# Hyena transforms by the time index modulo 4, with half the products, the lo parts of five weight streams by accumulating DMAs, and new DMA figures in the planner

## The chip, the cores and the metric

The kernel runs on one core of one Trainium2 chip. The metric is the device time of one execution in microseconds (us), the median over several runs. A core has TensorE (PE, with its weight loads shown as PEld), VectorE (DVE), ScalarE (ACT), GpSimd (POOL), SyncE (SP), whose queue issues the transfers, and 16 DMA engines.

## The reference, cut to what matters

Two transformer blocks run one after the other on 512 tokens of width 1024. The first block has neighbourhood attention, a Hyena mixer, a gated merge and a SwiGLU; the second has latent attention, a state-space branch, cross attention, a gated merge and a convolved SwiGLU. The change touches the Hyena mixer. Its long convolution is a product in the frequency domain, twice in a row (orders 0 and 1), over 512 tokens and 512 channels:

```python
def long_conv_bidir(u, h_fwd, h_bwd, bias):
    B, L, C = u.shape
    k2 = jnp.concatenate([h_fwd, jnp.zeros((1, C), jnp.float32), h_bwd[:0:-1]], axis=0)
    U = jnp.fft.rfft(u.astype(jnp.float32), n=2 * L, axis=1)
    K = jnp.fft.rfft(k2, n=2 * L, axis=0)
    y = jnp.fft.irfft(U * K[None], n=2 * L, axis=1)[:, :L]
    return (y + u.astype(jnp.float32) * bias.astype(jnp.float32)).astype(u.dtype)
...
    for n in range(HY_ORDER):
        z = gates[n] * long_conv_bidir(z, filt[:, 0, n], filt[:, 1, n], bias[n])
```

The projections around it are `h @ w_in` (its columns for the Hyena inputs are `w_hy` in the kernel, those of the two gates `w_gna` and `w_ghy`, those of the context's keys `w_kvc`) and `y_hy @ w_hy_o` (`w_hyo`).

## The kernel before, in words

**Numbers in two parts.** Every weight and activation is held as a hi part, rounded to fp32r by a copy on ACT, and a lo part, the original minus hi, made by a subtraction on DVE (`split` L783, `lo` L778). A product is three matmuls: hi by hi, hi by lo, lo by hi (`mm` L788). Weights come through `stream` (L797): one 512 KB load brings a group of 8 blocks of 128x128, which is then split into two tiles of 128x1024; `proj` takes 8 blocks (24 matmuls) for one output tile of 128x512 when the input has 1024 rows.

**The planner.** The code does not issue instructions as it goes. `Trace.add` records every call with its operands, a duration (`Trace.time` L479) and what it depends on. `Trace.plan` (L691) runs a list scheduler (`schedule` L542) over the five queues, forward and backward by turns, with the figures of `LAG` (L246: how long after one engine's end another can start), `RELEASE` and the DMA rate at L495, and with 48 page pairs of 128x512 floats (`PAGES` L32) as a limited resource. The order of the best pass is what `emit` (L707) writes out. So the figures set the order in every queue of the whole program, and no instruction waits for a planned time: it waits for semaphores alone.

```python
LAG = (
...
    (1500.0, 2000.0, 1000.0, 1300.0, 2250.0),
)
...
        return max(450.0, out.size() * 4 / 360.0)
```

The last row of `LAG` is a DMA before PE, DVE, ACT, POOL and another DMA, in ns; 360 is GB/s. All transfers go out from SP's queue.

**Hyena** (`hyena` L1195). 12 tiles of 128 channels are projected with `w_hy` and run through a short convolution (`short_conv`, whose tile has two edge columns set to zero by memsets on POOL). `to_time` (L1206) turns four of them with PE into time on the partitions. Times are split by parity: p is the time modulo 2, hh the half. For each order and each half of the channels, `order` (L1237) computes, for both halves kt of the 256 odd frequencies, cosine (j=0) and sine (j=1) sums of the even and the odd times: 2 p x 2 j x 2 hh x 3 = 24 matmuls of 256 columns per kt. A sum and a difference of the two banks give frequencies k and 511-k; they are multiplied with the filters' spectrum, which `filters` (L1107) has stored in DRAM, added and subtracted once more and split. The inverse takes 48 matmuls per half. In order 0 time lies on the partitions of the result; in order 1 the operands are exchanged, so that channels do, and the gate is multiplied in two strided pieces per tile.

**What stands around it.** `hyena` is mixed with the rest of the filters, the context's keys and values (`context` L1323) and the first gate (`gate_na` L1513); after it `neighbourhood` (L1433) is mixed with `branch_hy` (L1524), which takes `w_ghy` and `w_hyo`. In the profile every instruction has line L714, the one in `emit` that issues it, so rows are told apart by engine, form and time. By the times of their loads, the filters lie in 0 to 75 us, Hyena in 75 to 220, the neighbourhood attention in 220 to 430, the merge in 430 to 560, the first feed-forward in 560 to 900, the second block's branches and merge in 900 to 1320, its feed-forward in 1320 to the end.

Of the kernel before, what the change touches and what calls it, by code (L numbers as in the profile page):

```python
# [15 lines left out]
F32 = mybir.dt.float32  # L16
# [8 lines left out]
P = 128  # L25
# [99 lines left out]
def _constants():  # L125
    c = {}
    perm = _token_perm()
    inv = (np.float32(10000.0) ** (-np.arange(16, dtype=np.float32) / np.float32(16))).astype(np.float32)
    rc, rs = np.zeros((P, T), np.float32), np.zeros((P, T), np.float32)
    for p in range(P):  # L130
        d = p % 64
        pos = (perm // 64 if d < 32 else perm % 64).astype(np.float32)
        ang = (pos * inv[d % 16]).astype(np.float64)
        rc[p] = np.cos(ang)
        rs[p] = np.sin(ang) * (-1.0 if d % 32 < 16 else 1.0)
    c["rope1"] = np.concatenate([rc, rs], 1)

    i, k = np.arange(256)[:, None], np.arange(256)[None]
    w = np.pi * (2 * k + 1) / 1024.0
    ce, co, se, so = np.cos(w * 2 * i), np.cos(w * (2 * i + 1)), np.sin(w * 2 * i), np.sin(w * (2 * i + 1))  # L140
    c["dft"] = np.concatenate(
        [m.astype(np.float32).reshape(2, P, 256).transpose(1, 0, 2).reshape(P, 512) for m in (ce, se, co, so, ce.T, se.T)], 1)
# [7 lines left out]
    c["zfeat"] = np.ascontiguousarray(z.T)  # L150
# [3 lines left out]
    tt = np.array([[2 * (hh * P + np.arange(P)) + p for hh in range(2)] for p in range(2)]).reshape(4, P)  # L154
    c["inv2"] = np.tile((f(10000.0) ** (-np.arange(0, 32, 2, dtype=f) / f(32))).astype(f)[None], (P, 1))
    c["cmask"] = np.where(np.arange(P)[None] <= np.arange(P)[:, None], 0.0, NEG).astype(f)
    c["eye16"] = np.tile(np.eye(16, dtype=f), (2, 1))
    c["decay"] = np.ascontiguousarray(decay[tt].transpose(1, 0, 2)).reshape(P, 4 * T)
    return c


def layout(inp):
# [88 lines left out]
    (1500.0, 2000.0, 1000.0, 1300.0, 2250.0),  # L251
# [4 lines left out]
RELEASE = 200.0, 150.0, 150.0, 100.0, 1200.0  # L256
TABLES = {AF.Silu: (0,), AF.Sin: (1, 0), AF.Exp: (2,), AF.Gelu_apprx_tanh: (3,)}
# [75 lines left out]
class Call:  # L333
    __slots__ = ("engines", "engine", "name", "args", "kw", "time", "rank", "deps", "then", "waits", "pieces", "begun", "urgent", "start", "number", "tables", "columns", "ports")
# [128 lines left out]
class Trace:  # L463
# [41 lines left out]
    def add(self, engines, name, args, kw):  # L505
# [25 lines left out]
        c.tables = TABLES.get(args[2]) if name == "activation" else None  # L531
        deps.discard(c.number)
# [9 lines left out]
    def schedule(self, order, back=False):  # L542
# [36 lines left out]
        while left or events:  # L579
# [78 lines left out]
            while events and events[0][0] <= now:  # L658
# [13 lines left out]
                if kind == 0:  # L672
                    idle[c.engine] = True
                    for j in c.deps if back else c.then:
                        d = calls[j]
                        gap = LAG[d.engine][c.engine] if back else LAG[c.engine][d.engines[0]]
                        n += 1
                        push(events, (now + gap, n, 2, j))
                    if not back and c.pieces:
                        n += 1  # L680
                        push(events, (now + RELEASE[c.engine], n, 1, i))
                    if not back:
                        continue
# [23 lines left out]
    def emit(self):  # L707
        at = lambda x: x.placed() if isinstance(x, View) else x
        for c in sorted(self.calls, key=lambda c: (c.start, c.number)):
# [3 lines left out]
            f = getattr(getattr(self.nc, ENGINES[c.engine]), c.name)  # L713
# [4 lines left out]
class Program:  # L718
# [78 lines left out]
    def stream(self, ap):  # L797

        for gi in range(ap.shape[0]):
# [3 lines left out]
            self.split((wh, wl), raw)  # L803
# [303 lines left out]
    def filters(self):  # L1107
# [8 lines left out]

        self.dft = lambda j, i, c0, n: tuple(w[:, i * 256 + c0 : i * 256 + c0 + n] for w in dft[j])
# [33 lines left out]
        for o in range(2):  # L1151
            for j in (1, 0):
# [17 lines left out]
                for kt in range(2):  # L1170
# [6 lines left out]
                    for r, op in enumerate((ALU.add, ALU.subtract)):  # L1177
                        K = self.u2()
                        V.tensor_tensor(out=K, in0=e, in1=O, op=op)
# [15 lines left out]
    def hyena(self):  # L1195
        nc, a = self.nc, self.a
        V = nc.vector
        blocks = self.stream(a["w_hy"])
# [38 lines left out]
        def order(o):  # L1237
            for half in range(2):
                zt = zT[half]
                PQ = []  # L1240
                for kt in range(2):
# [3 lines left out]
                    banks = []  # L1245
                    for p in range(2):
                        ps = self.psum("s")
                        for j in range(2):
                            for hh in range(2):
                                q = p * 2 + hh  # L1250
                                self.mm(ps[:, j * 256 : j * 256 + 256], self.dft(2 * p + j, hh, kt * P, P), tuple(z[:, q * 256 : q * 256 + 256] for z in zt), hh == 0, hh == 1)
                        banks.append(ps)
                    e = self.u2()
                    nc.scalar.copy(e, banks[0])
# [11 lines left out]
                    V.tensor_tensor(out=S[:, 1], in0=Yv[:, :, 0], in1=Yv[:, :, 1], op=ALU.subtract)  # L1266
                    d = (self.u4(dt=F32R), self.u4(dt=F32R))
                    self.split(d, T1)
                    PQ.append(d)
                    yield  # L1270
                pq = lambda p, j, kt, c0, n: tuple(t[:, p * 512 + j * 256 + c0 : p * 512 + j * 256 + c0 + n] for t in PQ[kt])
                inv = lambda p, j, kt, c0, n: self.dft(2 + j if p else 4 + j, kt, c0, n)
                if o == 0:
                    zn = (self.u4(dt=F32R), self.u4(dt=F32R))
                    zT[half] = zn
                    for p in range(2):
                        ps = self.psum("mm")
                        for hh in range(2):
                            n = 0
                            for j in range(2):  # L1280
                                for kt in range(2):
                                    self.mm(ps[:, hh * 256 : hh * 256 + 256], inv(p, j, kt, hh * P, P), pq(p, j, kt, 0, 256), n == 0, n == 3)
                                    n += 1
# [5 lines left out]
                else:  # L1289
                    for c in range(2):  # L1290
                        ct = half * 2 + c
                        ps = self.psum("mm")
                        for p in range(2):
                            n = 0
                            for j in range(2):
                                for kt in range(2):
                                    self.mm(ps[:, p * 256 : p * 256 + 256], pq(p, j, kt, c * P, P), inv(p, j, kt, 0, 256), n == 0, n == 3)
                                    n += 1
                        y = self.u2()
                        yv = y.rearrange("p (cb r c) -> p r cb c", cb=8, r=8)  # L1300
                        for p in range(2):
                            V.tensor_tensor(
                                out=yv[:, :, :, p : 8 : 2],
                                in0=ps[:, p * 256 : p * 256 + 256].rearrange("p (r cb c) -> p r cb c", r=8, cb=8),
                                in1=g2[ct][:, p : 512 : 2].rearrange("p (r cb c) -> p r cb c", r=8, cb=8),
# [17 lines left out]
    def context(self):  # L1323
# [4 lines left out]
        blocks = self.stream(self.a["w_kvc"])  # L1328
# [184 lines left out]
    def gate_na(self):  # L1513

        blocks = self.stream(self.a["w_gna"])
# [8 lines left out]
    def branch_hy(self):  # L1524

        nc = self.nc
        gb, ob = self.stream(self.a["w_ghy"]), self.stream(self.a["w_hyo"])
# [784 lines left out]
```

## Time and profile before

| what | us |
|---|---|
| median of 3 runs | 1740.57 (1739.26 to 1743.97) |
| the profiled execution's own time | 1740.42 |
| its span, first to last instruction | 1738.6 |
| PE busy | 1713.5 |
| DVE busy | 1176.4 |
| ACT busy | 714.2 |

The profile is of one execution. Busy times are unions of instructions on an engine; a matmul's end is modelled, so matmuls overlap in it and the pace is read from their starts.

### The profile page before, as it was taken

To read this page: it belongs to the slowest core of one execution; us is meant where nothing else is said; L and a number is where in the kernel's file an instruction comes from. 1 tells how busy PE (TensorE), PEld (TensorE's weight loads), DVE (VectorE), ACT (ScalarE), POOL (GpSimd) and SP (SyncE) were. 2 spreads that over 40 slices of the span, in tenths; PEclk is the share of its full clock that TensorE was granted. 3 is DMA by queue.
4 is the path that set the end of the run, shared out by engine and by line. 5 is a ranking of instruction groups with operands and counts; after the bars stand their busy time and mean duration, and the time that the engine had idled before them with its cause. 6 is when DMAs were issued, how large, how long until landed. Compare 5 with 4: busy or idle time off the path is not lost.

```text
span 1738.6 us, 22865 instructions
## 1 busy us (share of the span) xinstructions
PE 1713.5 (99%) x8494; PEld 1411.7 (81%) x8494; DVE 1176.4 (68%) x2452; ACT 714.2 (41%) x1185; POOL 29.0 (2%) x69
## 2 busy tenths in 40 slices
PE   7999999999999999999999999999999999999999
PEld 3589988888888888888888887888887888888887
DVE  6898976679997275453277947569987526896420
ACT  4544354566454122233162612556554313554310
POOL 0000000000000000000000000010100000000000
PEclk9999999999999999999999999999999999999999
DMA  9535323437963235323255355402356321222420
GB/s 343 171 124 170 108 88 99 144 117 256 353 231 115 80 106 173 110 73 121 73 187 179 131 171 148 132 35 93 113 191 230 110 85 61 85 73 85 144 93 19
DMA packets 93661, 235.41 MB, mean 135 GB/s; under 512 B 18316, under 2 KB 26252, under 8 KB 93550
## 3 DMA queue, kind: packets, MB, share of 16 engines
q1 hardware_dynamic: 93550, 233.95, 40.3%
q8 instruction: 67, 1.10, 0.3%
q14 instruction: 44, 0.36, 0.1%
HBM read 206.91 MB, written 27.00 MB: 135 GB/s over the span
## 4 chain that ended last, share of the span: by engine, by line
PE 89%; DVE 6%; DMA 2%; ACT 2%; issue 1%; SPq 0%; ACTq 0%; DVEq 0%
PE banks L714 89%; DVE pages L714 4%; ACT pages L714 2%; DVE small L714 1%; SPq L714 0%; DMA pages<-in_w_ada_dram 0%; DMA pages<-in_w_hyo_dram 0%; DMA pages<-in_w_out_dram 0%; DMA br<-pages 0%; DVE banks L714 0%; DMA pages<-s5w 0%; DMA ud<-pages 0%; DVE R L714 0%; ACTq L714 0%; DVEq L714 0%
## 5 line engine op out<-in xcount | busy, mean ns | idle before, releaser
L714 PE MATMUL banks<-pages,pages 128*128 128x512 f32 (+5 forms) x7769 | 1639.3, 370 | 9.2 <-DVE pages L714 7.8
L714 PEld LDWEIGHTS banks<-pages,pages 128*128 128x128 f32 (+1 forms) x7769 | 1335.1, 186 | 273.4 <-DVE pages L714 14.5
L714 DVE TENSOR_TENSOR pages<-pages,pages 128x1024 fp32r<-128x1024 f32 (+10 forms) x718 | 593.1, 855 | 100.6 <-ACT pages L714 69.5
L714 ACT CAST pages<-pages 128x1024 fp32r<-128x1024 f32 (+4 forms) x455 | 382.0, 865 | 337.6 <-PE banks L714 102.3
L714 DVE TENSOR_TENSOR pages<-banks,pages 128x512 fp32r<-128x512 f32 (+7 forms) x219 | 111.9, 523 | 99.8 <-PE banks L714 76.8
L714 ACT ACTIVATE pages<-banks 128x512 f32<-128x512 f32 (+4 forms) x75 | 37.5, 513 | 234.1 <-PE banks L714 222.9
L714 DVE TENSOR_TENSOR pages<-banks,R 128x512 f32<-128x512 f32 x81 | 57.1, 707 | 111.5 <-PE banks L714 111.4
L714 DVE TENSOR_TENSOR pages<-pages,banks 128x512 f32<-128x512 f32 x66 | 44.0, 681 | 98.4 <-PE banks L714 89.9
L714 ACT ACTIVATE pages<-pages 128x512 f32<-128x512 f32 (+4 forms) x91 | 50.8, 571 | 145.3 <-DVE pages L714 126.8
L714 ACT COPY pages<-banks 128x512 f32<-128x512 f32 (+5 forms) x119 | 58.5, 507 | 99.7 <-PE banks L714 89.5
L714 ACT ACTIVATE pages<-pages,vec 128x512 f32<-128x512 f32 (+1 forms) x84 | 63.0, 768 | 72.5 <-DVE pages L714 67.7
L714 DVE SCALAR_TENSOR_TENSOR pages<-pages,vec,pages 128x511 f32<-128x511 f32 (+3 forms) x114 | 82.6, 746 | 3.4 <-ACT pages L714 2.7
L714 PE MATMUL banks<-ident,pages 128*128 128x128 f32 (+2 forms) x464 | 70.1, 272 | 1.3 <-ACT pages L714 1.0
L714 PEld LDWEIGHTS banks<-ident,pages 128*128 128x128 f32 (+2 forms) x464 | 55.2, 143 | 15.9 <-ACT pages L714 6.0
L714 ACT CAST pages<-banks 128x512 fp32r<-128x512 f32 (+5 forms) x118 | 53.5, 473 | 26.8 <-PE banks L714 20.2
L714 ACT ACTIVATE pages<-banks,small 128x512 f32<-128x512 f32 (+3 forms) x80 | 46.7, 589 | 25.8 <-DVE small L714 21.3
L714 POOL MEMSET pages<- 128x1 f32 (+4 forms) x63 | 28.4, 476 | 1197.2 <-DVE pages L714 641.2
L714 DVE SCALAR_TENSOR_TENSOR pages<-pages,pages 128x1024 bf16<-128x1024 f32 (+3 forms) x42 | 42.8, 1020 | 2.4 <-DMA gna<-pages 1.2
L714 DVE SCALAR_TENSOR_TENSOR pages<-banks,mod,pages 128x512 f32<-128x512 f32 x16 | 11.7, 745 | 46.1 <-PE banks L714 46.1
L714 PE MATMUL banks<-pages,small 128*2 128x512 f32 x64 | 30.9, 617 | 7.0 <-DMA pages<-in_w_ada_dram 7.0
L714 DVE TENSOR_TENSOR pages<-pages 128x16 f32<-128x16 f32 (+6 forms) x120 | 34.5, 321 | 0.3
L714 DVE SCALAR_TENSOR_TENSOR pages<-pages,banks 128x512 f32<-128x512 f32 x40 | 27.1, 682 | 5.9 <-PE banks L714 5.7
(73 smaller groups left out, 412.8 us busy)
## 6 DMA issues: line engine op xcount, KB each, us to landing
pages<-in_w_f_dram SPq DMA_DIRECT2D x66, 512.0 KB, 3.8
pages<-in_w_ada_dram SPq DMA_DIRECT2D x48, 512.0 KB, 7.2
pages<-in_w_up_dram SPq DMA_DIRECT2D x44, 512.0 KB, 3.4
pages<-in_w_g_dram SPq DMA_DIRECT2D x24, 512.0 KB, 4.1
pages<-in_w_down_dram SPq DMA_DIRECT2D x22, 512.0 KB, 4.2
pages<-in_w_out_dram SPq DMA_DIRECT2D x16, 512.0 KB, 7.8
pages<-in_w_hy_dram SPq DMA_DIRECT2D x12, 512.0 KB, 4.7
pages<-in_w_na_dram SPq DMA_DIRECT2D x12, 512.0 KB, 3.3
```

The source lines that it names most:

```text
L714: self.tc.keep_in_program_order(f(*map(at, c.args), **{k: at(v) for k, v in c.kw.items()}))
```

## The change

Times are now split modulo 4. Of the forward transform only frequencies k below 128 are multiplied out; the sums and differences of the four residues give 127 others of the 512 from each (255-k, 256+k, 511-k). So A holds the sums and Dm the differences of the two banks per parity, and X is put together from them for kt = 0 and kt = 1. Before the inverse, the two halves are added and subtracted (`even`, `odd`), split, and multiplied with a quarter matrix. Order 1 now gets time on the partitions and is copied, turned by four transposes per tile, and gated in four strided pieces.

`stream(ap, True)` makes the lo part in another way: ACT writes hi, then -hi into the lo tile, and a DMA from the GpSimd queue reads the weights from DRAM a second time and adds them to it. It is used for `w_hy` (12 groups), `w_kvc` (4), `w_gna` (8), `w_ghy` (8) and `w_hyo` (4).

The planner's DMA figures change: 310 in place of 360 GB/s, a last row of `LAG` of 2200 to 2600 ns, and for an accumulating DMA 180 GB/s and 3000 ns more.

```diff
+    w = np.pi * (2 * k + 1) / 1024.0
+    m = [f(w * (4 * j[:, None] + 2 * h + p)) for p in range(2) for f in (np.cos, np.sin) for h in range(2)]
+    m += [f(w[:, :P] * (4 * j[:, None] + s)).T for f in (np.cos, np.sin) for s in range(4)]
...
-    (1500.0, 2000.0, 1000.0, 1300.0, 2250.0),
+    (2200.0, 2200.0, 2200.0, 2200.0, 2600.0),
...
+SUM_RATE, SUM_LAG = 180.0, 3000.0
...
-        return max(450.0, out.size() * 4 / 360.0)
+        return max(450.0, out.size() * 4 / (SUM_RATE if "accum_op" in kw else 310.0))
...
-            f = getattr(getattr(self.nc, ENGINES[c.engine]), c.name)
+            f = getattr(getattr(self.nc, "gpsimd" if c.late else ENGINES[c.engine]), c.name)
...
-            self.split((wh, wl), raw)
+            if dma:
+                self.nc.scalar.copy(wh, raw)
+                self.nc.scalar.activation(wl, wh.bitcast(F32), AF.Copy, scale=-1.0)
+                self.nc.sync.dma_start(out=wl, in_=ap[gi].bitcast(F32R), accum_op=ALU.add)
+            else:
+                self.split((wh, wl), raw)
...
-                self.transpose(ps[:, q * P : q * P + P], u[:, hh * 256 + p : hh * 256 + p + 255 : 2])
+                self.transpose(ps[:, q * P : q * P + P], u[:, 2 * hh + p : 2 * hh + p + 509 : 4])
...
+                A, Dm = [], []
+                for p in range(2):
+                    b = []
+                    for hh in range(2):
+                        ps = self.psum("s")
+                        for j in range(2):
+                            q = p * 2 + hh
+                            self.mm(ps[:, j * 256 : j * 256 + 256], self.dft(2 * p + j, hh, 0, P), tuple(z[:, q * 256 : q * 256 + 256] for z in zt), True, True)
+                        b.append(ps)
+                    e, s_, d_ = self.u2(), self.u2(), self.u2()
+                    nc.scalar.copy(e, b[0])
+                    V.tensor_tensor(out=s_, in0=e, in1=b[1], op=ALU.add)
+                    V.tensor_tensor(out=d_, in0=e, in1=b[1], op=ALU.subtract)
...
-                    V.tensor_tensor(out=X[:, :512], in0=e, in1=banks[1], op=ALU.add)
-                    V.tensor_tensor(out=X[:, 512:], in0=e, in1=banks[1], op=ALU.subtract)
+                    if kt == 0:
+                        V.tensor_tensor(out=X[:, :512], in0=A[0], in1=A[1], op=ALU.add)
+                        V.tensor_tensor(out=X[:, 512:], in0=A[0], in1=A[1], op=ALU.subtract)
+                    else:
+                        c0, s0, c1, s1 = (d[:, i * 256 : i * 256 + 256] for d in Dm for i in range(2))
+                        V.tensor_tensor(out=X[:, 0:256], in0=c0, in1=s1, op=ALU.add)
+                        V.tensor_tensor(out=X[:, 256:512], in0=c1, in1=s0, op=ALU.subtract)
+                        V.tensor_tensor(out=X[:, 512:768], in0=c0, in1=s1, op=ALU.subtract)
+                        V.tensor_tensor(out=X[:, 768:], in0=c1, in1=s0, op=ALU.add)
...
+                V.tensor_tensor(out=ends(even), in0=two(lower[:, :512]), in1=ends(upper), op=ALU.add)
+                V.tensor_tensor(out=two(even[:, 256:768]), in0=two(lower[:, :512]), in1=ends(upper), op=ALU.subtract)
+                V.tensor_tensor(out=odd[:, :512], in0=lower[:, 512:], in1=upper[:, 256:768], op=ALU.add)
+                V.tensor_tensor(out=odd[:, 512:], in0=lower[:, 512:], in1=upper[:, 256:768], op=ALU.subtract)
...
+                    for hh in range(2):
+                        for j in range(2):
+                            self.mm(ps[:, hh * 256 : hh * 256 + 256], inv(p, hh, j), pq(p, hh, j), j == 0, j == 1)
...
+                    for p in range(2):
+                        z = self.u2()
+                        nc.scalar.copy(z, times(p))
...
+                        for q in range(4):
+                            self.transpose(ps[:, q * P : q * P + P], zs[q // 2][:, q % 2 * 256 + c * P : q % 2 * 256 + c * P + P])
...
-        blocks = self.stream(a["w_hy"])
+        blocks = self.stream(a["w_hy"], True)
```

Beside these, the decay and the features of the filters are put into the new order of time, and one of the filters' subtractions exchanges its operands.

## Rows read from the trace of the kernel before

**Rows 1.** The page: span, and busy time of the engines.
```profile
span 1738.6 us, 22865 instructions
## 1 busy us (share of the span) xinstructions
PE 1713.5 (99%) x8494; PEld 1411.7 (81%) x8494; DVE 1176.4 (68%) x2452; ACT 714.2 (41%) x1185; POOL 29.0 (2%) x69
```
**Rows 2.** The page: the chain that ended last, by engine.
```profile
PE 89%; DVE 6%; DMA 2%; ACT 2%; issue 1%; SPq 0%; ACTq 0%; DVEq 0%
```
**Rows 3.** Windows by stage: length, busy us (instructions) per engine, clock, DMA share, GB/s.
```profile
core 0: us, PE busy (x) PEld busy (x) DVE busy (x) ACT busy (x) POOL busy (x), PEclk, DMA share, GB/s
75.00:220.00 145.00, 145.00 (x881) 130.14 (x882) 135.49 (x206) 61.00 (x95) 2.27 (x12) 1.00 0.44 139
220.00:430.00 210.00, 209.55 (x1089) 176.55 (x1089) 156.82 (x333) 117.63 (x222) 4.92 (x12) 1.00 0.40 135
...
1450.00:1500.00 50.00, 50.00 (x222) 41.20 (x221) 38.67 (x53) 22.29 (x31) 0.00 (x0) 1.00 0.22 74
```
**Rows 4.** Timeline of PE: start us, us, what, in two stretches of the Hyena stage.
```profile
181.73 5.42 PE L714 MATMUL banks<-pages,pages 128*128 128x256 f32 x44
...
158.87 0.63 PE L714 MATMUL banks<-ident,pages 128*128 128x128 f32 x4
159.25 0.47 PE L714 MATMUL banks<-pages,pages 128*128 128x512 f32 x1
```
**Rows 5.** Groups by form on PE, 75 to 220 us: count, busy us, mean ns, idle.
```profile
L714 PE MATMUL banks<-pages,pages 128*128 128x256 f32 x477 | 60.7, 283 | 0.0
```
**Rows 6.** Groups by form on DVE, 75 to 220 us; the last from 220 to 430.
```profile
L714 DVE TENSOR_TENSOR pages<-pages,pages 128x1024 fp32r<-128x1024 f32 x30 | 36.0, 1216 | 0.0
...
L714 DVE TENSOR_TENSOR pages<-pages,banks 128x512 f32<-128x512 f32 x24 | 15.6, 678 | 7.0 <-PE banks L714 7.0
L714 DVE TENSOR_TENSOR pages<-pages,pages 128x512 f32<-128x512 f32 x16 | 10.4, 683 | 0.0
...
L714 DVE TENSOR_SCALAR pages<-pages,vec 128x512 f32<-128x512 f32 x12 | 6.5, 540 | 0.6 <-ACT pages L714 0.5
...
L714 DVE TENSOR_TENSOR pages<-pages,pages 128x256 f32<-128x256 f32 x6 | 2.5, 419 | 0.0
L714 DVE TENSOR_TENSOR pages<-banks,pages 128x256 f32<-128x256 f32 x6 | 2.5, 419 | 0.2 <-PE banks L714 0.2
...
L714 DVE TENSOR_TENSOR pages<-banks,pages 128x192 fp32r<-128x192 f32 x8 | 2.8, 352 | 1.0 <-ACT pages L714 0.9
```
**Rows 7.** Groups by form on ACT: the whole span, then 75 to 220 us.
```profile
L714 ACT ACTIVATE pages<-pages 128x1024 f32<-128x1024 f32 x2 | 2.1, 1058 | 0.0
...
L714 ACT COPY pages<-banks 128x512 f32<-128x512 f32 x22 | 12.9, 587 | 39.2 <-PE banks L714 35.0 <-DVE pages L714 4.2
```
**Rows 8.** POOL's instructions: duration ns min/median/max, first and last start us, forms.
```profile
L714 POOL MEMSET pages<- x63: 99/308/1236, 0.7 to 1225.6; 128x1 f32 x24, 32x1024 f32 x16, 64x256 f32 x10, 64x512 f32 x8
```
**Rows 9.** Landing of 512 KB loads: those of w_hy, then those of w_out.
```profile
DMA to landing us min/median/max: 3.2/4.7/7.8
...
DMA to landing us min/median/max: 3.6/7.8/10.9
```
**Rows 10.** Windows around two waits of the second block; columns as in rows 3.
```profile
1060.00:1074.00 14.00, 12.09 (x59) 9.15 (x57) 13.99 (x14) 1.34 (x2) 0.00 (x0) 0.99 0.34 97
1074.00:1080.60 6.60, 5.32 (x21) 4.35 (x22) 6.49 (x7) 2.25 (x4) 0.00 (x0) 0.50 0.73 227
...
1295.00:1306.00 11.00, 9.01 (x40) 7.13 (x38) 5.41 (x8) 1.85 (x3) 0.00 (x0) 1.00 0.95 338
1306.00:1312.70 6.70, 4.93 (x12) 3.91 (x13) 5.79 (x7) 4.80 (x5) 0.00 (x0) 0.50 0.83 303
```
**Rows 11.** The chain that ended last, pieces of DMA at both waits: start us, us, what.
```profile
1050.01 4.90 DMA pages<-s5w
...
1291.49 5.88 DMA br<-pages
...
1298.26 6.53 DMA pages<-in_w_out_dram
```

More of the change, by code (lines that the diff above doesn't have):

```diff
@@ L153, in _constants @@
     decay = np.exp((-t * deltas).astype(f).astype(np.float64)).astype(f) * f(1.0 / 512)
-    tt = np.array([[2 * (hh * P + np.arange(P)) + p for hh in range(2)] for p in range(2)]).reshape(4, P)
+    tt = np.array([[4 * np.arange(P) + 2 * hh + p for hh in range(2)] for p in range(2)]).reshape(4, P)
     c["inv2"] = np.tile((f(10000.0) ** (-np.arange(0, 32, 2, dtype=f) / f(32))).astype(f)[None], (P, 1))
@@ L333 @@
 class Call:
-    __slots__ = ("engines", "engine", "name", "args", "kw", "time", "rank", "deps", "then", "waits", "pieces", "begun", "urgent", "start", "number", "tables", "columns", "ports")
+    __slots__ = ("engines", "engine", "name", "args", "kw", "time", "rank", "deps", "then", "waits", "pieces", "begun", "urgent", "start", "number", "tables", "columns", "ports", "late")
 class Arena:
@@ L531, in add @@
         c.tables = TABLES.get(args[2]) if name == "activation" else None
+        c.late = SUM_LAG if "accum_op" in kw else 0.0
         deps.discard(c.number)
@@ L675, in schedule @@
                         d = calls[j]
-                        gap = LAG[d.engine][c.engine] if back else LAG[c.engine][d.engines[0]]
+                        gap = LAG[d.engine][c.engine] + d.late if back else LAG[c.engine][d.engines[0]] + c.late
                         n += 1
@@ L680, in schedule @@
                         n += 1
-                        push(events, (now + RELEASE[c.engine], n, 1, i))
+                        push(events, (now + RELEASE[c.engine] + c.late, n, 1, i))
                     if not back:
@@ L795, in mm, with stream @@
         self.pe += 3 * out.ap.free_size() / 2.4
-    def stream(self, ap):
+    def stream(self, ap, dma=False):
         for gi in range(ap.shape[0]):
@@ L1178, in filters @@
                         K = self.u2()
-                        V.tensor_tensor(out=K, in0=e, in1=O, op=op)
+                        if r and j and kt:
+                            V.tensor_tensor(out=K, in0=O, in1=e, op=op)
+                        else:
+                            V.tensor_tensor(out=K, in0=e, in1=O, op=op)
                         self.load(self.spec[o][kt][:, r, j], K)
@@ L1266, in order, with times @@
                     V.tensor_tensor(out=S[:, 1], in0=Yv[:, :, 0], in1=Yv[:, :, 1], op=ALU.subtract)
+                    S_.append(T1)
+                    yield
+                lower, upper = S_
+                even, odd = self.u4(), self.u4()
+                ends = lambda t: t.rearrange("p (i c) -> p i c", i=4)[:, 0:4:3]
+                two = lambda t: t.rearrange("p (i c) -> p i c", i=2)
+                V.tensor_tensor(out=ends(even), in0=two(lower[:, :512]), in1=ends(upper), op=ALU.add)
+                V.tensor_tensor(out=two(even[:, 256:768]), in0=two(lower[:, :512]), in1=ends(upper), op=ALU.subtract)
+                V.tensor_tensor(out=odd[:, :512], in0=lower[:, 512:], in1=upper[:, 256:768], op=ALU.add)
+                V.tensor_tensor(out=odd[:, 512:], in0=lower[:, 512:], in1=upper[:, 256:768], op=ALU.subtract)
+                PQ = []
+                for t in (even, odd):
                     d = (self.u4(dt=F32R), self.u4(dt=F32R))
-                    self.split(d, T1)
+                    self.split(d, t)
                     PQ.append(d)
-                    yield
-                pq = lambda p, j, kt, c0, n: tuple(t[:, p * 512 + j * 256 + c0 : p * 512 + j * 256 + c0 + n] for t in PQ[kt])
-                inv = lambda p, j, kt, c0, n: self.dft(2 + j if p else 4 + j, kt, c0, n)
+                yield
+                at = lambda p, hh, j: (2 * hh + j if p else 2 * j + hh) * 256
+                pq = lambda p, hh, j: tuple(t[:, at(p, hh, j) : at(p, hh, j) + 256] for t in PQ[p])
+                inv = lambda p, hh, j: self.dft(4 + j, hh, p * P, P)
+                def times(p):
+                    ps = self.psum("mm")
+                    for hh in range(2):
+                        for j in range(2):
+                            self.mm(ps[:, hh * 256 : hh * 256 + 256], inv(p, hh, j), pq(p, hh, j), j == 0, j == 1)
+                    return ps
                 if o == 0:
@@ L1276, in order @@
                     for p in range(2):
[L1277 to L1283, printed above, removed]
+                        ps = times(p)
                         z = self.u2()
@@ L1327, in context @@
         yield
-        blocks = self.stream(self.a["w_kvc"])
+        blocks = self.stream(self.a["w_kvc"], True)
         self.kc, self.vc = [], []
@@ L1513, in gate_na @@
     def gate_na(self):
-        blocks = self.stream(self.a["w_gna"])
+        blocks = self.stream(self.a["w_gna"], True)
         self.gna = self.scratch("gna")
@@ L1526, in branch_hy @@
         nc = self.nc
-        gb, ob = self.stream(self.a["w_ghy"]), self.stream(self.a["w_hyo"])
+        gb, ob = self.stream(self.a["w_ghy"], True), self.stream(self.a["w_hyo"], True)
         self.bhy = self.scratch("bhy")
```

45 lines of the change are left out of this document (18 added, 27 removed).

## The prediction, made before the changed kernel was run

> **What bounds the kernel now.** I read the page's head, then the chain that ended last, then the windows by stage, then the forms inside the stage that changes. The head says that TensorE (PE) is busy 1713.5 of 1738.6 us [rows 1], and the chain runs 89% through PE [rows 2]. A busy PE need not be a full one, so the reader should look at the pace: 222 products of 512 columns in 50 us of the second feed-forward are 225 ns each [rows 3], and in the Hyena stage 44 products of 256 columns stand in 5.42 us [rows 4]; less the 0.28 us that the last one takes [rows 5], that is 5.14 / 43 = 0.1195 us from start to start. They follow one another without idle time. In 75 to 220 us, where Hyena lies, PE is busy for all of 145.00 us, but VectorE (DVE) is at 135.49 and ScalarE (ACT) at 61.00 [rows 3]: PE is the bound, with DVE close behind. In 220 to 430 us DVE has 156.82 of 210 us and ACT 117.63 [rows 3]. The order on each queue comes from the planner at build time, so freed PE time is filled by whatever is ready, the gate projections for instance.
>
> **PE.** Per half and order the forward transform goes from 48 products to 24 and the inverse from 48 to 24: four times 96 become four times 48, so 192 of 384 go. The stage shows 477 products of this width [rows 5], which is these and the 96 of the context keys, some records missing. The remaining ones keep their form (128x128 by 256 columns, three passes), so 192 x 0.1195 = 22.9 us go. Order 1 now comes out with time on the partitions and has to be turned: 4 tiles x 4 = 16 transposes more. Four of them start at 158.87 and the next product at 159.25 [rows 4], so 0.095 us each, 1.5 us. The 32 transposes into time read every fourth column in place of every second; the trace has no such stride; bounds are nothing and a doubling, 32 x 0.095 = 3 us. I take nothing, as the columns per transpose stay the same. PE: -22.9 + 1.5 = **-21.4 us**, on the path, since PE is never idle there.
>
> **DVE.** Halving the products costs additions. Per half, four sums with a bank (0.678 us) were needed; now there are four with a bank, two of 512 columns (0.683), four of 256 (0.419) and four of 512 (0.683): 8.5 us in place of 2.7, +5.8 us, four times = +23. Order 1's gating is four pieces of 128 columns in place of two of 256 (0.419); each is at most the 0.352 of 192 columns, so at most +0.6 x 4 = +2.3. Together +25 us [rows 6]. Taking lo by DMA removes a subtraction of 1.216 us for each of 36 groups (12 of w_hy, 4 of w_kvc, 8 of w_gna, 8 of w_ghy, 4 of w_hyo): -43.8 us. Net -19 us over 75 to 430 us. But in 75 to 220 us only the 16 groups of w_hy and w_kvc surely fall, -19.5, so DVE stands at 135.5 + 25 - 19.5 = 141 us against 145 - 21.4 = 123.6 us of PE. The 17 us are hidden only if PE draws work from the next stage; the w_gna and w_ghy streams are 16 groups x 24 x 0.225 = 86 us of PE that now need no DVE for their weights. I cost the excess at nothing for that reason; if that cover is gone, it is the last rival.
>
> **ACT.** Each of the 36 groups gains a pass that writes -hi, of the form that takes 1.058 us, and order 1 four copies from a bank (0.587): 38 + 2 = +40 us [rows 7]. About 19 of them fall before 220 us (61 becomes 80 of 145) and 21 after (118 becomes 139 of 210). It is hidden in ACT's idle time.
>
> **The added transfers and their queue.** 36 accumulating DMAs of 512 KB leave from POOL's queue, 19 MB in all. The trace has none. POOL ran 63 memsets, all short [rows 8]; an issue costs at least little and at most about its longest, 1.24 us: 45 us in some 330, hidden. On that queue each DMA waits for ACT's -hi, and behind it stand the memsets: the short convolutions' edges (24 of 128x1) and the zero halves of keys, on which DVE and then PE wait. Each lo group now reaches PE through load, two ACT passes and a second transfer. The planner's new figures allow 2.9 us (180 GB/s) + 3.0 + 2.2 = 8.1 us for it. Plain loads of this size land in 3.2 to 10.9 us [rows 9]; I bound an accumulate by one plain load at its best, 3.2, and two at the worst, 21.8. Against 8.1 that is nothing late, or 13.7 us late. I take nothing: the end of one plain load is the nearer row, as w_hy's own loads have a median of 4.7 us, and even two of these make 9.4, 1.3 over the planner's figure, while the other streams' groups give PE 5.4 us each (24 x 0.225) to cover it.
> From rows, DVE does not run double speed in this stage: its one-source TENSOR_SCALAR takes 540 ns for 512 columns [rows 6]. The Trainium skill speaks against the change here: SBUF — State Buffer, section "SBUF: two separate sides", says that descriptors of a DMA issued from GpSimd can't be written while VectorE runs an instruction in a two-port mode. By that rule each accumulate could start late by one DVE instruction; no run here shows it. What it would give stands with the rivals.
>
> The other edits (the reordered columns of the transform matrices, the decay and the features, the swapped operands of a subtraction) change no instruction's form; I cost them at nothing, with nothing to cover.
>
> **The planner's DMA figures.** They move every queue's order, in all stages. Where the old ones were most wrong PE stood: before 1074 us it is idle 14.00 - 12.09 = 1.9 us and then 1.3, with 5.32 us of work at a granted clock of 0.50 (1.2 GHz), which costs half of them, 2.7; around 1306 us 2.0 + 1.8 idle and 2.5 at 0.50 [rows 10]. Together 12.1 us. The chain there hangs on a load of s5w (4.90), a store to br (5.88) and a load of w_out (6.53 us) [rows 11]. For that last load the old figures say 1.46 + 1.0 = 2.5 us, the new ones 1.7 + 2.2 = 3.9: a third of the 4.1 us that lacked. So I take a third of 12.1: **-4 us**. Bounds: -12 (both waits go), and +12 (a changed order makes two like them elsewhere).
>
> **Sum.** The profiled execution took 1740.4 us (1738.6 span, 1.8 around it); the median of the runs, 1740.57, is 0.2 above it, so no correction. 1740.4 - 21.4 - 4 = **1715 us**. With transposes at +3 and the order off by up to 8 us either way, this case's own range is 1707 to 1725.
>
> **Rivals.**
> - The new order removes both waits of the second block: 1740.4 - 21.4 - 12 = 1707. For it: both hang on landings that the planner took too short. Against it: around 1306 us the merge leaves PE little else to do.
> - The accumulates land late, slower than before. Place: the first group of each of the five streams, where no earlier group covers it. At two crowded loads (2 x 7.8 [rows 9]) against 8.1 a start is 7.5 us late: 5 x 7.5 = 37.5, so 1740.4 - 21.4 + 37.5 = 1757. It decides from 21.4 / 36 = 0.6 us late per group on average. For it: PE's queue is in order, POOL's too, and the trace has no price. Against it: DMA is only 0.40 to 0.44 busy from 75 to 430 us [rows 3].
> - Each accumulate starts late behind the DVE instruction that runs when it is issued. DVE is busy 93% of the stage, and its longest form takes 1.216 us [rows 6]; with no cover at all 36 x 1.22 = 44 us are on the path: 1715 + 44 = 1759, decided from the same 0.6 us. Against it: loads of other groups run ahead. The rule of the Trainium skill named above would be its cause.
> - DVE becomes the bound of the Hyena stage: the stage takes DVE's 141 us, not PE's 123.6, so 4 us of 145 are won: 1736. For it: longer DVE chains between transform and inverse, DVE at 93% now. Against it: 86 us of PE work without weights on DVE.
>
> **How the numbers follow.** The forecast 0.58 (1715); both waits gone 0.16 (1707); DVE as the bound 0.12 (1736, half of it within, half faster); late accumulates 0.09 (1757); accumulates held by DVE 0.03 (1759); the whole-program order gives the gain back 0.02 (1740). A measurement of this kernel tells 0.3% (5 us) from no change. Faster by over that: 0.58 + 0.16 + 0.06 = 0.80; within: 0.06 + 0.02 = 0.08; slower: 0.09 + 0.03 = 0.12. The range leaves out both cases of late accumulates and the tail of the best order: 1702 to 1737.
>
> **What would show it.** Right: products of 256 columns down by 192 and 0.12 us apart; transposes up by 16; DVE subtractions of 1024 columns down by 36; 36 DMAs from POOL; PE idle time in 75 to 430 us still near nothing; ACT +40 us. Wrong: PE waiting for in_w_hy, in_w_gna or in_w_hyo through POOL's DMAs; PE waiting for DVE between 90 and 200 us; granted clock below 1.00 in 75 to 430 us; new low-clock stretches after 560 us.

## The result, and the profile after

The changed kernel takes 1721.48 us (median of 4 runs, 1719.19 to 1722.21) beside 1739.91 for the kernel before: a ratio of 0.9892 with a 95% interval of 0.9879 to 0.9905, or 19 us less. The forecast was 1715 in a range of 1702 to 1737: the direction and the range held, and the gain fell some 6.5 us short of the forecast.

The page of the changed kernel: its head, the chain by engine, and the DMA queues.
```profile
span 1720.4 us, 22736 instructions
## 1 busy us (share of the span) xinstructions
PE 1689.9 (98%) x8318; PEld 1390.7 (81%) x8318; DVE 1156.4 (67%) x2464; ACT 745.2 (43%) x1220; POOL 60.6 (4%) x105
...
q1 hardware_dynamic: 93550, 233.95, 40.4%
q0 software_dynamic: 5184, 18.88, 6.3%
...
PE 93%; DVE 4%; DMA 1%; issue 1%; ACT 1%; SPq 0%; DVEq 0%; ACTq 0%
```
Beside [rows 1], PE is busy 23.6 us less and the span is 18.2 us shorter, so PE's idle time has grown by 5.4 us, from 25.1 to 30.5. DVE is down by 20.0, ACT up by 31.0, POOL up by 31.6 us. The chain runs through PE for 93% of the span, 89% before [rows 2].

Where PE stood idle, in the windows of before that [rows 3] did not hold (the start and the second block), and then those of the changed kernel; columns as in [rows 3].
```profile
0.00:75.00 75.00, 63.39 (x211) 28.46 (x211) 54.68 (x106) 37.67 (x63) 1.81 (x24) 1.00 0.77 271
...
900.00:1320.00 420.00, 410.60 (x2266) 342.16 (x2265) 323.51 (x923) 202.42 (x408) 19.07 (x20) 0.98 0.44 144
```
```profile
0.00:75.00 75.00, 59.52 (x198) 28.64 (x199) 44.83 (x94) 34.80 (x56) 5.40 (x28) 1.00 0.89 281
75.00:220.00 145.00, 142.86 (x780) 122.85 (x779) 141.00 (x241) 98.48 (x147) 21.61 (x37) 1.00 0.88 229
220.00:430.00 210.00, 207.77 (x1104) 175.94 (x1102) 150.63 (x351) 124.18 (x231) 13.66 (x19) 1.00 0.60 181
...
900.00:1320.00 420.00, 413.89 (x2246) 345.25 (x2245) 312.61 (x812) 198.07 (x402) 18.93 (x20) 1.00 0.44 140
```
The reader should read idle time as length minus PE's busy time, and keep in mind that the windows are fixed in time: in the faster kernel each of them holds a little more of the work that comes next. The start has lost 3.9 us (15.5 idle in place of 11.6), the Hyena stage 2.1, the stage behind it 1.8. The second block has won: 6.1 idle in place of 9.4, and its mean granted clock is 1.00 in place of 0.98, as the low-clock stretch and the wait around 1306 us [rows 10] are gone. The stretch near 1074 us is shorter but still there: the 3.20 us from 1076.40 on run at a granted clock of 0.50. In 75 to 220 us DVE stands at the 141 us that were worked out, on 145 us with PE busy for 142.86: the two are now nearly equally full there. The mean DMA share of that stage has doubled, from 0.44 to 0.88.

The groups that the change touches, by form over the whole span: first the products of 256 columns and the transposes of before, then those of the changed kernel with the passes on ACT and the transfers on POOL.
```profile
L714 PE MATMUL banks<-pages,pages 128*128 128x256 f32 x1028 | 147.7, 286 | 0.3 <-ACT pages L714 0.2
L714 PE MATMUL banks<-ident,pages 128*128 128x128 f32 x380 | 59.0, 276 | 1.3 <-ACT pages L714 1.0
```
```profile
L718 PE MATMUL banks<-pages,pages 128*128 128x256 f32 x838 | 126.0, 288 | 8.1 <-ACT pages L718 6.0 <-DVE pages L718 1.9
L718 PE MATMUL banks<-ident,pages 128*128 128x128 f32 x396 | 61.3, 276 | 4.7 <-ACT pages L718 3.8 <-DVE pages L718 0.8
...
L718 ACT ACTIVATE pages<-pages 128x1024 fp32r<-128x1024 f32 x36 | 38.3, 1063 | 0.6
...
L718 POOL DMA_DIRECT2D pages<-in_w_hy_dram x12 | 10.8, 900 | 129.0 <-DMA spec<-pages 51.2 <-ACT pages L718 44.6 <-DVE pages L718 21.4
```
190 of the 192 products are seen to be gone (some records are missing), and 16 transposes are there. The landing times of the accumulates, in the list of DMA issues (x count, KB, median us from issue to landing):
```profile
pages<-in_w_hy_dram POOLq DMA_DIRECT2D x12, 512.0 KB, 7.3
pages<-in_w_gna_dram POOLq DMA_DIRECT2D x8, 512.0 KB, 7.8
pages<-in_w_ghy_dram POOLq DMA_DIRECT2D x8, 512.0 KB, 6.1
pages<-in_w_kvc_dram POOLq DMA_DIRECT2D x4, 512.0 KB, 8.2
pages<-in_w_hyo_dram POOLq DMA_DIRECT2D x4, 512.0 KB, 7.9
```

### The profile page after: what moved, and what is told of

Read it like the earlier page. It is cut to its first block, busy times and chain, and to the rows that moved or that the text cites. A ratio compares the mean times of both kernels' runs of the same rounds, so it can differ in the third digit from the quotient of the medians.

```text
span 1720.4 us, 22736 instructions
## 1 busy us (share of the span) xinstructions
PE 1689.9 (98%) x8318; PEld 1390.7 (81%) x8318; DVE 1156.4 (67%) x2464; ACT 745.2 (43%) x1220; POOL 60.6 (4%) x105
## 3 DMA queue, kind: packets, MB, share of 16 engines
q1 hardware_dynamic: 93550, 233.95, 40.4%
## 4 chain that ended last, share of the span: by engine, by line
PE 93%; DVE 4%; DMA 1%; issue 1%; ACT 1%; SPq 0%; DVEq 0%; ACTq 0%
PE banks L718 93%; DVE pages L718 3%; ACT pages L718 1%; DVE small L718 1%; DMA pages<-in_w_ada_dram 0%; DMA pages<-in_memT_dram 0%; DMA pages<-in_dft_dram 0%; DVE banks L718 0%; SPq L718 0%; DVEq L718 0%; ACTq L718 0%
## 5 line engine op out<-in xcount | busy, mean ns | idle before, releaser
L718 PE MATMUL banks<-pages,pages 128*128 128x512 f32 (+4 forms) x7576 | 1616.5, 373 | 13.4 <-ACT pages L718 8.4
L718 PEld LDWEIGHTS banks<-pages,pages 128*128 128x128 f32 (+1 forms) x7576 | 1311.8, 185 | 274.4 <-ACT pages L718 15.3
L718 DVE TENSOR_TENSOR pages<-pages,pages 128x512 f32<-128x512 f32 (+12 forms) x747 | 576.5, 804 | 82.8 <-ACT pages L718 72.5
L718 DVE TENSOR_TENSOR pages<-banks,pages 64x256 f32<-64x256 f32 (+7 forms) x229 | 114.3, 519 | 103.2 <-PE banks L718 79.9
L718 ACT ACTIVATE pages<-pages 128x512 f32<-128x512 f32 (+5 forms) x127 | 88.7, 709 | 139.0 <-DVE pages L718 121.8
L718 PE MATMUL banks<-pages,small 128*2 128x512 f32 x64 | 28.8, 606 | 5.1 <-DMA pages<-in_w_ada_dram 5.1
L718 DVE TENSOR_REDUCE small<-banks 128x1 f32<-128x256 f32 (+3 forms) x64 | 27.9, 447 | 0.1
```

The costliest lines, as they stand in the source:

```text
L718: self.tc.keep_in_program_order(f(*map(at, c.args), **{k: at(v) for k, v in c.kw.items()}))
```

## The experiments

The change has three parts: the transforms, lo by DMA, and the planner's figures. Every combination of them was run, then parts of the second and third, then the price of the accumulates by itself.

### The transforms alone

The switches of this run, on the changed kernel; the combinations below turn the same ones. The figure lines are taken back, and each of the five streams loses its `True`:

```diff
-    (2200.0, 2200.0, 2200.0, 2200.0, 2600.0),
+    (1500.0, 2000.0, 1000.0, 1300.0, 2250.0),
...
-        return max(450.0, out.size() * 4 / (SUM_RATE if "accum_op" in kw else 310.0))
+        return max(450.0, out.size() * 4 / (SUM_RATE if "accum_op" in kw else 360.0))
...
-        blocks = self.stream(a["w_hy"], True)
+        blocks = self.stream(a["w_hy"])
```

> The modulo-4 transforms alone: all lo parts by DVE's subtraction, the DMA figures of before. Theory P (the gain is PE work, 192 products of 0.1195 us less 16 transposes): 1740 - 21 = 1719 us, even without the lo parts by DMA, as the planner can draw PE work from the next stage. Rival D (DVE has no room for the added sums in 75 to 220 us): DVE would need 135.5 + 25 = 160 us where PE needs 124, so little of the gain stays: 1732 to 1755 us, DVE busy for all of 75 to 220 us and PE idle there by 5 us or more. Rival F (the gain is the new figures' order): 1736 or more.

Measured: 1742.51 us, ratio 1.0016 (1.0007 to 1.0025): 2.8 us slower, with 192 products fewer. Theory P falls for this combination. Rivals D and F both allow the time; DVE's and PE's rows are those of D, and F falls with the figures alone, below. Windows of this kernel: the stage, and the stretch in it where PE stood longest.
```profile
75.00:220.00 145.00, 133.67 (x703) 112.88 (x701) 143.39 (x232) 60.99 (x98) 2.00 (x10) 0.96 0.39 130
...
200.00:216.00 16.00, 9.50 (x43) 7.71 (x42) 16.00 (x27) 4.60 (x9) 0.00 (x0) 0.68 0.19 69
```
PE's waits between 75 and 230 us (in total, times, longest), and the chain there (start us, us, what):
```profile
PE banks L718 <- DVE pages L718: 7.7, 7, 4.1
PE banks L718 <- ACT pages L718: 4.0, 7, 0.7
```
```profile
180.95 6.12 DVE pages L718 x10
...
187.58 7.21 DVE pages L718 x11
...
205.35 4.83 DVE pages L718 x7
...
216.65 3.90 DVE pages L718 x7
```
DVE is busy for 143.39 of 145 us and the chain runs on it from 175 to 220 us. PE is idle for 11.3 us of the stage where it was never idle before. Around its longest wait, 4.1 us up to 207.2, the granted clock is 0.68 on the mean of 16 us, so some 10 of them ran at 1.2 GHz. What the products gave back went into waits and a low clock.

### Lo by DMA alone

> The lo parts of the five streams by accumulating DMAs alone, old transforms, old DMA figures for plain transfers (180 GB/s and 3 us for the accumulates). Theory P: PE work is the same, so 1740 us within 5; DVE -44 us, ACT +38, POOL +31. Rival D would see PE gain where DVE was full: 1730 to 1735. If accumulates land late for PE: 1745 or more, with PE waiting behind POOL's DMAs.

The streams keep their `True`, the transforms and the figures are those of before. Measured: 1743.70 us, ratio 1.0023 (1.0013 to 1.0032), 4 us slower. The start and the Hyena stage of this kernel:
```profile
0.00:75.00 75.00, 59.46 (x193) 26.68 (x194) 48.72 (x99) 39.30 (x62) 6.19 (x27) 0.98 0.90 293
75.00:220.00 145.00, 145.00 (x827) 127.67 (x826) 100.13 (x164) 75.67 (x117) 16.16 (x30) 1.00 0.69 184
```
This is theory P's time (1740 within 5). In the stage DVE falls to 100.13 of 145 us and PE gains nothing, as it was already full. What is lost is lost in the first 75 us, where DMA is 0.90 busy: PE is busy for 59.46 in place of 63.39 us. In that kernel's chain a load of ctxT, 3.41 us on the chain from 62.86 us on, stands ahead of PE.

### The figures alone

> The new DMA figures alone (310 GB/s, 2.2 to 2.6 us). Theory P with my estimate: 1736 us, since about a third of 12.1 us of waits in the second block goes. From the trace of the change: waits in 900 to 1320 us less by some 9 us, the start worse by some 4: 1735 us. Rival F: 1725 or less.

Measured: 1738.96 us, ratio 0.9996 (0.9986 to 1.0006): no difference that can be told, so rival F falls. Its windows:
```profile
0.00:75.00 75.00, 61.07 (x201) 26.99 (x202) 52.46 (x102) 33.67 (x59) 1.74 (x22) 1.00 0.83 285
...
900.00:1320.00 420.00, 413.23 (x2298) 346.13 (x2298) 328.85 (x930) 203.07 (x411) 19.17 (x20) 1.00 0.45 146
```
The second block gains as in the changed kernel (6.8 idle in place of 9.4, clock 1.00), and the start gives 2.3 us of it back.

### The transforms and lo by DMA

> Transforms and lo by DMA, old DMA figures. Theory P: 1719 us, 4 over or under the sum of the two alone. Rival F: 1730 or more. Rival D: well under the transforms alone (by 10 us or more), since only here DVE has room.

Measured: 1722.81 us, ratio 0.9905 (0.9890 to 0.9920). Neither of the two gains anything alone, together they take 17 us off: DVE in 75 to 220 us is at 134.15, PE at 142.33 us. Theory P's figure was right here (1719 within 4), and so was rival D's condition: 19.7 us under the transforms alone.

### The transforms with the figures; lo with the figures

> Transforms and new DMA figures, no lo by DMA. If DVE's room in the Hyena stage is what the products lack: no gain again, 1735 to 1745, DVE busy over 140 of 145 us in 75 to 220 and PE waiting for DVE there. If the loss of the transforms alone was an accident of one order: 1719 to 1725.

Measured: 1735.50 us, ratio 0.9976 (0.9966 to 0.9985). Its Hyena stage:
```profile
75.00:220.00 145.00, 133.42 (x701) 111.59 (x700) 143.76 (x233) 65.81 (x105) 2.39 (x14) 0.98 0.39 131
```
It is the picture of the transforms alone, with another order, and as expected for a DVE without room: DVE at 143.76 us, PE idle for 11.6 us. A gain of 4 us is left all the same.

> Lo by DMA and new figures without the modulo-4 transforms: what the transforms are worth once DVE has room. If the 192 products carry the gain: 1738 to 1744, so that the transforms are worth 17 to 23 us beside the change's 1721. If lo by DMA and figures carry it: 1730 or less.

Measured: 1744.43 us, ratio 1.0021 (1.0011 to 1.0030), 0.4 us over the range for the case that the products carry the gain. All eight combinations, as the ratio to the kernel before:

| | old figures | new figures |
|---|---|---|
| neither | 1 | 0.9996 |
| transforms | 1.0016 | 0.9976 |
| lo by DMA | 1.0023 | 1.0021 |
| both | 0.9905 | 0.9892 |

With lo by DMA, the transforms are worth 1.0023 - 0.9905 = 1.18%, 20.5 us, or 1.0021 - 0.9892 = 1.29%, 22.4 us with the new figures: around the 21.4 that were worked out. Without it they are worth -2.8 and 3.5 us.

As each kernel has its own order, and orders alone differ by many us (below), the reader should compare all orders of one kind. With the transforms, the four kernels with lo by DMA for all five streams take 1718.7 to 1732.1 us, the two with a part of the streams 1733.8 and 1734.1, the two without 1735.5 and 1742.5. The kinds do not overlap.

### Half of the streams by DMA

> The change with lo by DMA for w_hy and w_kvc only (16 groups; w_gna, w_ghy and w_hyo are split by DVE again). If DVE's relief inside the stage decides (19.5 us of subtractions gone from 75 to 220 us): 1720 to 1724, most of the gain stays. If the gate streams, PE work without DVE work for weights, are what fills PE: 1732 to 1738.

```diff
-        blocks = self.stream(self.a["w_gna"], True)
+        blocks = self.stream(self.a["w_gna"])
...
-        gb, ob = self.stream(self.a["w_ghy"], True), self.stream(self.a["w_hyo"], True)
+        gb, ob = self.stream(self.a["w_ghy"]), self.stream(self.a["w_hyo"])
```

> The change with lo by DMA for w_gna, w_ghy and w_hyo only (20 groups; w_hy and w_kvc split by DVE). The other way round: if relief inside the stage decides, 1732 to 1738; if the gate streams as filler decide, 1720 to 1724. If both serve, each alone gives about 1725 to 1730.

Here the first `stream` of `hyena` and that of `context` lose their `True`, and the others keep it. Measured: 1734.13 us, ratio 0.9968 (0.9958 to 0.9979), with w_hy and w_kvc alone; 1733.81 us, ratio 0.9965 (0.9953 to 0.9976), with the gates and w_hyo alone. Their Hyena stages, in this order:
```profile
75.00:220.00 145.00, 139.56 (x748) 119.18 (x746) 134.79 (x229) 80.72 (x125) 13.94 (x26) 0.99 0.72 192
```
```profile
75.00:220.00 145.00, 137.46 (x716) 116.73 (x716) 138.61 (x227) 71.77 (x117) 8.32 (x22) 0.98 0.50 144
```
Each time lies in the range in which the other half decides, so neither half is the cause alone. Each keeps about a third of the gain, hardly more than the 0.9976 of no lo by DMA at all. PE is idle for 5.4 and 7.5 us of the stage, at a mean clock under 1.00, where the whole change has 2.1. The start is worse in both as well, with PE busy for 56.52 and 56.82 of the first 75 us in place of 59.52; some 3 of the 12 us are lost there and not in the stage. So both serve, and not in proportion; their exact shares stay open.

### The price of the accumulates

> The change without the 36 accumulating DMAs: the lo tiles of the five streams keep -hi, so the weights are not added to them and the products with them are not the reference's. DVE's relief and ACT's extra pass stay, the transfers, POOL's issues and their latency go. If the accumulates' latency and DMA load cost PE time: 1708 to 1715. If they are hidden: 1721 within 5, the same PE work with other waits.

```diff
-                self.nc.sync.dma_start(out=wl, in_=ap[gi].bitcast(F32R), accum_op=ALU.add)
```

Measured: 1721.26 us, ratio 0.9889 (0.9874 to 0.9904), against 0.9892 with the 36 transfers. POOL is back at 28.8 us, and the DMA share in 75 to 220 us at 0.45:
```profile
75.00:220.00 145.00, 144.84 (x764) 124.23 (x765) 128.38 (x216) 84.15 (x125) 2.66 (x14) 0.99 0.45 150
```
In the sum, the transfers, their issues and their latency cost nothing that can be told. But this kernel has an order of its own, and PE's idle time is elsewhere: 16.7 us in the start, at a mean clock of 0.95, and 0.2 from 75 to 430 us, where the change has 15.5 and 4.4. So this holds for the sum, not for each wait.

### The order's chance

> The change with the planner's plain DMA rate back at 360 GB/s, the longer latencies kept. If the rate is what reorders the first loads and keeps PE idle some 4 us longer before 75 us: 1717 to 1719, the first 50 us as before. If the latencies do it: 1721 within 2.

> The change with the planner's plain DMA rate at 312 in place of 310 GB/s, so small a shift that only the order's chance can differ. If an order's chance is worth little: 1721 within 2. If the 360 GB/s run showed chance and not the rate: anywhere from 1718 to 1732.

The only edit of either is the number 310.0. Measured: 1732.12 us at 360 GB/s, ratio 0.9956 (0.9941 to 0.9971); 1718.69 us at 312, ratio 0.9874 (0.9858 to 0.9891). At 360 the start is as before (PE busy for 62.96 of 75 us), as the first theory had it, and yet the kernel is 11 us slower than the change, which neither expectation allowed. PE is not idle for longer (29.7 us beside 30.5); its busy time for the same products is 13.0 us up. Low-clock stretches at 74, 903 and 1313 us account for some of it, the rest stays open. At 312 it is the fastest of all that ran: its four executions (1716.86 to 1719.11) lie below the four of the change, though the intervals of the two ratios overlap. That fits the case that chance and not the rate made the other run's time. Its first three stages:
```profile
0.00:75.00 75.00, 62.37 (x203) 27.67 (x204) 48.53 (x98) 39.31 (x63) 5.40 (x28) 1.00 0.84 266
75.00:220.00 145.00, 143.94 (x779) 123.31 (x778) 140.69 (x241) 91.23 (x137) 21.69 (x38) 1.00 0.88 237
220.00:430.00 210.00, 209.87 (x1134) 179.12 (x1133) 149.15 (x346) 132.57 (x242) 13.14 (x18) 1.00 0.61 186
```
PE is idle there for 12.6, 1.1 and 0.1 us, where the change has 15.5, 2.1 and 2.2. That a lone figure moves the whole by 13 us means that a difference of a few us between two orders says nothing of the parts that made them. One wait does go with the figure: between 1280 and 1335 us PE is idle for 2.5 to 3.8 us in all five kernels planned with 360 GB/s (before, the transforms alone, lo alone, the two together, and the 360 run), and for 0.7 us or less in all nine with 310 or 312. Whether 360 as such is bad beyond that, or its order unlucky, was not settled.

### More of the same in the second block

> The change with lo by DMA for 34 more groups, the gate and output streams of the second block (w2_g0 to w2_g2, and w2_o1, w2_o2 at half the rows). DVE -41 us where it has 312 of 420 us. If PE's waits between 900 and 1320 us come from a full DVE: 1712 to 1718. If they come from chains of short operations and from landings: 1721 within 4.

```diff
-        blocks = self.stream(self.a[f"w2_g{j}"])
+        blocks = self.stream(self.a[f"w2_g{j}"], True)
...
-        gb, ob = self.stream(self.a[f"w2_g{j}"]), self.stream(self.a[f"w2_o{j}"])
+        gb, ob = self.stream(self.a[f"w2_g{j}"], True), self.stream(self.a[f"w2_o{j}"], True)
```

The trace shows 32 such groups, 24 and 8, and not the 34 of the text. Measured: 1729.67 us, ratio 0.9939 (0.9924 to 0.9954), 8 us slower than the change and outside both expected ranges. Its second block:
```profile
900.00:1320.00 420.00, 410.65 (x2222) 343.03 (x2221) 280.35 (x799) 223.48 (x426) 44.21 (x49) 0.99 0.65 181
```
DVE falls from 312.61 to 280.35 us, and PE is idle for 9.4 us in place of 6.1. So DVE's relief buys nothing there; what the 8 us come from, and how much of them is the order's chance, stays open.

## Why the prediction was right or wrong

**PE.** The mechanism was right: -21.4 us were worked out, and 20.5 and 22.4 measured, given lo by DMA. That both lie within 1 us of it is in part luck, as the order alone moves the kernel by more. The trace bears the size out: PE's busy time fell by 23.6 us, and by estimate 3.5 of them are clock. Before, 5.32 + 4.93 us of PE's work in the second block ran at 0.50 [rows 10], now 3.20 us do, and half of the difference is 3.5. Some 20 us are left for the transforms. The transposes keep their mean of 276 ns, with the other stride and with 16 more.

**DVE.** The sum over the kernel was right, -20.0 us where -19 stood. That the stage shows 141.00 us, as worked out, is in part luck: other orders of the same parts have 134.15 (old figures), 136.74 (360) and 140.69 us (312) in this window. One bound was too low: the gating pieces of 128 columns take 0.400 us in the stage (mean of seven), not at most 0.352, which makes 0.8 us in all. Costing DVE's excess over PE at nothing was right for the change as it is: PE waits for DVE for 1.8 us in the stage. The reason given, that PE draws work from streams which need no DVE, shows in the loads of w_gna, before and after (ns, then first and last start in us):
```profile
L714 SPq DMA_DIRECT2D pages<-in_w_gna_dram x8: 328/328/382, 149.4 to 318.9; - x8
```
```profile
L718 SPq DMA_DIRECT2D pages<-in_w_gna_dram x8: 327/330/575, 153.8 to 199.3; - x8
```
All eight groups now come within the Hyena stage; with the transforms and without lo by DMA the last one leaves at 306.8 (old figures) or 237.7 us (new). The 17 us of excess had that cover as their condition: taking lo by DMA away costs 19.7 us with the old figures and 14.0 with the new, taking either half of the streams back some 12. The last rival (1736, DVE as the bound) is thus what the kernel does without lo by DMA: 1742.5 and 1735.5. That the second is so near is no proof of the rival's sum, which had DVE relieved of 16 groups.

**ACT.** +40 us were worked out; the 36 passes take 38.3 and the copies rise by four, yet the total is only 31.0 up. Table loads account for most of the rest: 14 before, 9 after, of 1283 ns each, 6.4 us. Their number goes by the order: four kernels with the same parts have 9, 12, 13 and 14. Some 3 us stay open. It was hidden, as said.

**The added transfers.** Nothing for their latency is borne out: PE's products wait for no transfer from 75 to 560 us, its weight loads for one of w_hy, 0.3 us, and the run without them takes the same time, though in another order. At 312, with all 36 of them, PE is idle for no more than 1.2 us from 75 to 430. They land after 6.1 to 8.2 us (medians), close to the planner's 8.1, and inside the bounds of 3.2 and 21.8. POOL's issues take 0.86 to 1.11 us each, under the bound of 1.24:
```profile
L718 POOL DMA_DIRECT2D pages<-in_w_hy_dram x12: 862/862/1112, 53.6 to 161.5; - x12
```
The two rivals of late accumulates did not come. DVE is busy 97% of this stage, and yet the median issue takes as little as the shortest, and none in the row lasts longer than a DVE instruction of 1.22 us. The rule of the Trainium skill that spoke against the change (SBUF — State Buffer, section "SBUF: two separate sides") is not contradicted by that, as its condition, a two-port mode, does not show in the rows; no run here tests it.

**The planner's figures.** The term put -4 us, a third of two waits in the second block. There the mechanism was right and the size too small: the wait around 1306 us is gone as a whole, and goes with the rate of 360 GB/s in all runs, while the one near 1074 stays. The second block has 3.3 us less idle time, and with the 3.5 us of clock it gains 6.8.

**Where the prediction failed: PE's idle time outside the second block, put at nothing.** The step on the figures looked at the second block alone, while the same figures reorder the first loads too, and PE was costed as never idle from 75 to 430 us. Idle time grew by 3.9 us in the start and by 3.9 us from 75 to 430, where PE's waits are for DVE (2.9 us) and ACT (0.7). PE's waits in the first 75 us, before and after:
```profile
PE banks L714 <- DMA pages<-in_w_ada_dram: 7.0, 1, 7.0
PE banks L714 <- DMA pages<-in_hy_mlp_dram: 3.4, 1, 3.4
```
```profile
PE banks L718 <- ACT pages L718: 7.0, 2, 6.0
PE banks L718 <- DMA pages<-in_w_ada_dram: 5.1, 1, 5.1
PE banks L718 <- DMA pages<-in_hy_mlp_dram: 3.4, 1, 3.4
```
The first load of w_ada, the weights of the modulation, as the chain that ended last shows it, before and after (start us, us):
```profile
4.56 6.74 DMA pages<-in_w_ada_dram
```
```profile
8.97 7.76 DMA pages<-in_w_ada_dram
```
In the changed kernel's order a product of the filters stands ahead of the modulation on PE and waits 6.0 us for ACT to split its matrix. That is not the wait that counts, as it ends at 10.48 us. The first load of w_ada leaves 4.4 us later than before, and the modulation's first product starts at 16.77 in place of 11.44 us. All this happens before any accumulate has been issued (the first leaves at 53.6 us). At 312 the first load of w_ada leaves at 5.55 us; PE's idle time is 2.9 us less in the start and 3.2 less from 75 to 430 us than in the change, and the kernel is 2.8 us faster. So most of what was lost there belongs to one order and not to the parts; why the planner came to that order stays open.

By the runs, the figures are worth -0.7 us alone (-2.4 to +1.0), -7.0 beside the transforms, -0.3 beside lo by DMA and -2.3 beside both; -4 lies within that spread, and no run singles it out. Added one after another, lo by DMA (+4.0), the transforms (-20.5) and the figures (-2.3) make -18.8, where the sum had 0 - 21.4 - 4 = -25.4. The largest part of the gap is thus the 4.0 us of lo by DMA, which that run loses in the start. As the order alone moves more than any of these terms but the transforms, this is book-keeping and no proof.

Two slips in the sums change nothing here: the rival of 1757 leaves the -4 us of the figures out while that of 1759 keeps them, and the kernel's own range, with 3 and 8 us above 1715, ends at 1726.

## What to carry to other kernels

Work taken off the engine that bounds a stage is worth its time only as far as the next engine has room in that stage: compare what the second one needs after the change with what the first one needs, and if it is more, the relief belongs to the same change. Relief counts in the next stage too, where that stage's work can be drawn forward. Two parts that each measure as a small loss can be a gain together, so neither should be judged alone. Where an order is planned at build time, test a result against a slight shift of the planner's figures before explaining a few us by a cause.

## What was not expected of the hardware

- An accumulating transfer loads the DMA engines about twice as much as a plain one: 6.3% of 1720.4 us for 36 transfers is 3.0 us of all 16 engines for 512 KB each, while 40.4% for 233.95 MB is 1.56 us per 512 KB, on the mean of all plain transfers. That is why the share in the Hyena stage doubled to 0.88, as it is 0.45 without them. Plain loads of w_hy beside them landed after 6.6 us (median) in place of 4.7 [rows 9], and PE's products wait for none of them in the stage.
- Idle time of PE is paid twice at times: in the run with the transforms alone the granted clock around the longest wait of the stage, 4.1 us, is 0.68 over 16 us. Not each wait does it: the changed kernel has waits of 6.0 and 5.1 us in its first 17 us, at a granted clock of 1.00.
- Of the order rather than the hardware: a change of under 1% in one of the planner's figures moved the kernel by 2.8 us, and one of 16% by 11 us.
